# A final RMSNorm at the end of an encoder block: four output tiles scaled by token on ScalarE out of transposed banks, and the work around the last products reordered

## The chip, the core and the metric

The kernel runs on one core of one Trainium2 chip. The core has five engines with a program of their own each: TensorE (PE; its weight loads are PEld), VectorE (DVE), ScalarE (ACT), GpSimd (POOL) and SyncE (SP, which here only issues DMAs). Between engines they wait on semaphores. Sixteen DMA engines move data between HBM and the on-chip memory SBUF; matmuls write to PSUM, which the kernel uses as eight banks. The metric is the device time of one execution in microseconds (us), as the median of several runs.

## The reference

One layer of an encoder for 512 tokens of 2048 features in float32: attention and gated linear attention side by side, an output projection, a gated MLP with a convolution, and, at the end, an embedding gate and a final norm. Only this end matters here:

```python
        h = rms_norm(x, norm_ple_w[i])
        g = jax.nn.sigmoid(h @ w_ple_gate[i])
        x = x + g * (p[i] @ w_ple_proj[i])
    return rms_norm(x, final_norm_w)
```

`rms_norm` multiplies x by the inverse root of its mean square over the 2048 features of a token, and by a weight per feature. So nothing of the output can be scaled for good before the last feature of that token has been computed.

## The kernel before, in words

**Layout.** Features lie on the 128 partitions, tokens along the free dimension. Block m (0 to 7) holds features m·128 and (m+8)·128 onward as two rows s = 0, 1 of 512 tokens. The tokens are cut into a first half (`lo_half`, 0 to 255) and a second half (`hi_half`, 256 to 511).

**Products.** A projection is made of units, one for each block. Each unit is a 2x2 matrix product (two feature rows by two token halves), done with seven block products in Winograd's manner (`PRODUCTS`, L21): P1 and P2 give quarter C11 (row 0, first half), P5 and P7 C22, P6 and P3 C12 (row 0, second half), P4 C21. A float32 product is three passes of eight matmuls with rounded operands: high part by high part, high by low, low by high, 24 matmuls (`product`, L481). `prep_high` (L446) rounds the weights on ScalarE (`wh<-l`, `wh<-s`), `prep_low` (L469) takes the rest on VectorE (`wl<-`). The accumulator is a PSUM bank (accA for P1, P6, P7, P4; accB; accC for P5 and P3, banks handed on in a list by `bank`, L477). `collect` (L502) moves it into the unit's page u: a ScalarE copy for the first product of a quarter (`u<-accA`), a VectorE addition for the second (`u<-u,accC`).

**Order.** `steps` is the list of all products; in the main loop (L1262) step i first runs its agenda entries of key 0 and 1, then `prep_low` of a coming step, the product, the entries of key 2 and more, and then `collect`. Each entry is recorded through `InOrder` (L56), which holds every engine to the order of recording; that is why almost every instruction of the profile has line 64. `end` (L961) is the first of the last 14 steps: the seven products of units u6 and u7 in turn, of which the last four (P5 and P3 of each) are written out by hand behind the loop, from L1355.

**The end.** The last stage's projection is the embedding gate. A quarter is finished by `times_norm` (L947: VectorE multiplies by the earlier norm's root rb, ScalarE takes the sigmoid) and `add_gated` (L953: VectorE multiplies by the projected embedding `ppl` and adds to the residual xs, ScalarE squares into page q). The squares are added into `acc`. The blocks 0 to 5 have been stored to HBM (x3d) and are read back by `reload` (L928); `weigh` (L936) multiplies them by the final weight, two ScalarE instructions `x<-x,cols` a block, `weigh_part` (L1349) those of u6 and u7 by quarters. Final norm, for each token half: `sums_by_token` (L1301) sums acc and squares over the partitions with matmuls by ones (`ms`), `root_begin` and `root_end` (L1312, L1319) make the inverse root (`tok`: a ScalarE square root and small VectorE steps) with one token on each partition, and a diagonal matrix `dg`; `spread` (L1329) turns that into a row on all partitions by one matmul (`pb`). `finish` (L1340) multiplies a block's half by it on VectorE and writes 256 KB to the output. `keep_warm` (L1334) is matmuls whose result nobody reads (`pw`).

**Queues.** DMAs are issued by SP, ACT or POOL, each in the order of its own program; writes of the first half go by SP, of the second half by SP for odd and by ACT for even blocks.

Of the kernel before, what the change touches and what calls it, by code (L numbers as in the profile page):

```python
# [11 lines left out]
AF = mybir.ActivationFunctionType  # L12
ALU = mybir.AluOpType

P = 128
T = 512
# [25 lines left out]
def encoder_block(ctx: ExitStack, tc: tile.TileContext, A, out):  # L42
    nc = tc.nc
# [433 lines left out]
    def bank(name):  # L477
        tag = banks.pop(0)
        return tag, pp_.tile([P, T], F32, tag=tag, name=name)
# [444 lines left out]
    x3 = {}  # L924
# [3 lines left out]
    def reload(i):  # L928
        t = xtile(("R11", "R21")[i // 2], i % 2, "x3", F32)
        for j in range(2):  # L930
            m = 2 * i + j
            if m < 6:
                x3[m] = t[:, j, :].rearrange("p (s t) -> p s t", s=2)
                nc.sync.dma_start(x3[m], x3d[m])

    def weigh(m):  # L936
        for s in range(2):
            act.activation(x3[m][:, s, :], x3[m][:, s, :], AF.Copy, scale=nfin[:, m + 8 * s:m + 8 * s + 1])

    sq_page = {}  # L940
    both = slice(0, 2)
# [5 lines left out]
    def times_norm(unit, s, c):  # L947
        o = unit.o[:, s, c]
        r = rb[:, None, c].broadcast_to([P, 2, 256]) if isinstance(s, slice) else rb[:, c]
        vec.tensor_tensor(o, o, r, ALU.mult)  # L950
        act.activation(o, o, AF.Sigmoid)

    def add_gated(unit, s, c):  # L953
        o, xs = unit.o[:, s, c], unit.xs[:, s, c]
        vec.tensor_tensor(o, o, unit.pp[:, s, c], ALU.mult)
        vec.tensor_tensor(xs, xs, o, ALU.add)
        if unit not in sq_page:
            sq_page[unit] = spare("q").rearrange("p (s t) -> p s t", s=2)
        act.activation(sq_page[unit][:, s, c], xs, AF.Square)
# [2 lines left out]
    for n in range(2):  # L962
        agenda[end + 2].append((0, lambda n=n: reload(n)))
    agenda[end + 7].append((0, lambda: reload(2)))
    for m in range(4):
        agenda[end + 5 + m].append((2, lambda m=m: weigh(m)))

    for n in range(2):
        u = stages[-1].units[n - 2]
        agenda[end + 4 + 2 * n] += [(2, lambda u=u: times_norm(u, 0, lo_half))]  # L970
        agenda[end + 5 + 2 * n] += [(2, lambda u=u: add_gated(u, 0, lo_half))]
        agenda[end + 6 + 2 * n] += [(1, lambda u=u: vec.tensor_tensor(acc[:, lo_half], acc[:, lo_half], sq_page[u][:, 0, lo_half], ALU.add))]

    def mean_square(c):
        n = (c.stop - c.start) // P
# [325 lines left out]
    def sums_by_token(parts, ms=None, done=True):  # L1301

        first = ms is None
        if first:
            ms = psum_aux("ms")[:, :2]
        for n, q in enumerate(parts):
            for t in range(2):
                ten.matmul(ms[:, t:t + 1], q[:, t * P:t * P + P], ones[:, 0:1], start=first and n == t == 0,
                           stop=done and n == len(parts) - 1, skip_group_check=True)
        return ms  # L1310
# [20 lines left out]
        ten.matmul(pb, ones, dg, start=True, stop=True)  # L1331
        return pb

    def keep_warm(n):  # L1334
        t = bank("pw")
        banks.append(t[0])
        for _ in range(n):
            ten.matmul(t[1][:, :P], ones, ones, start=True, stop=True)

    def finish(c, r, ms):  # L1340
        for m in ms:
            t = x3[m][:, :, c]
            vec.tensor_tensor(t, t, r[:, None, :].broadcast_to([P, 2, 256]), ALU.mult)
            (nc.sync if m % 2 or c is lo_half else nc.scalar).dma_start(out2[m][:, :, c], t)

    u6, u7 = units[-2:]
    x3[6], x3[7] = u6.xs, u7.xs
# [1 line left out]
    def weigh_part(unit, ss, c):  # L1349
        for s in ss:  # L1350
            m = unit.u + 8 * s
            act.activation(unit.xs[:, s, c], unit.xs[:, s, c], AF.Copy, scale=nfin[:, m:m + 1])


    lo, hi = lo_half, hi_half  # L1355
    sq = lambda u, s, c: sq_page[u][:, s, c]
    ms, rs = {}, {}
    product(u6, "P5")
    times_norm(u7, 1, lo)
    collect(u6, "P5")  # L1360
    vec.tensor_tensor(acc[:, lo], acc[:, lo], sq(u6, 1, lo), ALU.add)
    add_gated(u7, 1, lo)
    product(u7, "P5")
    times_norm(u6, 1, hi)
    weigh_part(u6, range(2), lo)
    add_gated(u6, 1, hi)
    collect(u7, "P5")
    product(u6, "P3", 9, lambda: ms.update(lo=sums_by_token([acc[:, lo], sq(u7, 1, lo)])))
    times_norm(u7, 1, hi)
    w0 = root_begin(ms["lo"])  # L1370
    add_gated(u7, 1, hi)
    d0 = root_end(lo, *w0)
    weigh_part(u7, range(2), lo)
    collect(u6, "P3")
    product(u7, "P3", 10, lambda: rs.update(lo=spread(d0)))
    times_norm(u6, 0, hi)
    weigh(4)
    add_gated(u6, 0, hi)
    finish(lo, rs["lo"], (0, 1))
    collect(u7, "P3")  # L1380
    m1 = sums_by_token([acc[:, hi], sq(u6, 1, hi), sq(u7, 1, hi), sq(u6, 0, hi)], done=False)
    times_norm(u7, 0, hi)
    finish(lo, rs["lo"], (2,))
    keep_warm(8)
    add_gated(u7, 0, hi)
    act.activation(warm, ones[:, 0:1], AF.Sqrt)
    m1 = sums_by_token([sq(u7, 0, hi)], m1)
    finish(lo, rs["lo"], (3, 4))
    keep_warm(4)
    w1 = root_begin(m1)  # L1390
    d1 = root_end(hi, *w1)
    rs["hi"] = spread(d1)
    weigh(5)
    weigh_part(u6, (1, 0), hi)
    weigh_part(u7, (1, 0), hi)
    finish(lo, rs["lo"], (6,))
    finish(hi, rs["hi"], range(4))
    finish(lo, rs["lo"], (5,))
    finish(hi, rs["hi"], range(4, 8))
    finish(lo, rs["lo"], (7,))  # L1400


def _blocks(w):
# [59 lines left out]
```

## Time and profile before

| | us |
|---|---|
| median of 3 runs (2300.37 to 2307.55) | 2304.75 |
| the profiled execution | 2304.32 |
| its span, first to last instruction | 2302.6 |
| TensorE busy | 2261.4 (98%) |
| VectorE busy | 1888.0 (82%) |
| ScalarE busy | 1300.7 (56%) |
| matmuls, all engines' instructions | 18016, 44996 |

Times in rows of the profile count from the start of the span. The granted clock of TensorE is 0.99 of full on the mean. "Busy" counts the time in which an instruction is in the engine; an engine that waits for a semaphore isn't busy. A row of the timeline has start, length, engine, line, operation, what it writes and reads, shapes and the count of merged instructions, and in brackets how long the engine had stood idle before and who ended that. Instructions that follow each other overlap by some 0.1 us, so a row of two 128x512 scalings lasts less than twice one of them.

### The profile page before, as it was taken

The numbers are of one execution on the slowest core, as the hardware profiler recorded it, in microseconds if no ns is written. First come the engines' busy times: TensorE is split into PE (matmuls) and PEld (weight loads), VectorE is DVE, ScalarE is ACT, GpSimd is POOL, SyncE is SP. The second block draws the span as 40 slices with busy tenths as digits, with TensorE's granted clock in tenths as the row PEclk, the third lists the DMA queues.
The fourth block names the chain that finished last, engine by engine and source line by source line (L and its number), as shares of the span: only waits on it lengthen the run. The fifth ranks groups of instructions, "written<-read, shape, count | busy, mean of one in ns | idle before, by whom it ended". The sixth has DMA issues, their size and how long they took to land.

```text
span 2302.6 us, 44996 instructions
## 1 busy us (share of the span) xinstructions
PE 2261.4 (98%) x18016; PEld 2189.7 (95%) x18016; DVE 1888.0 (82%) x2590; ACT 1300.7 (56%) x1908; POOL 144.0 (6%) x181
## 2 busy tenths in 40 slices
PE   9999999999999999999999999999999999999996
PEld 8888889999989999999999999999999999999996
DVE  7566458998788888998888888888898787998986
ACT  6354456776565665555555555555564554656655
POOL 0000000000000100000000000000000100000000
PEclk9999999999999999999999999999999999999999
DMA  6623586667978977787878787777866967879994
GB/s 217 204 74 110 183 271 166 186 182 200 309 251 257 327 214 211 207 221 205 227 197 219 204 222 211 215 208 217 272 207 231 309 216 255 268 254 329 268 292 163
DMA packets 195569, 516.77 MB, mean 224 GB/s; under 512 B 20928, under 2 KB 72384, under 8 KB 195360
## 3 DMA queue, kind: packets, MB, share of 16 engines
q1 hardware_dynamic: 166080, 422.37, 52.5%
q0 software_dynamic: 23616, 84.95, 21.2%
q10 hardware_dynamic: 5664, 6.59, 0.8%
q8 instruction: 141, 2.31, 0.4%
q14 instruction: 68, 0.56, 0.1%
HBM read 435.18 MB, written 76.55 MB: 222 GB/s over the span
## 4 chain that ended last, share of the span: by engine, by line
PE 87%; DVE 6%; DMA 3%; ACT 3%; issue 2%; DVEq 0%; ACTq 0%; POOLq 0%; SPq 0%
PE accA L64 40%; PE accC L64 21%; PE accB L64 10%; PE v L252 3%; PE v L254 3%; PE v L253 3%; DVE wl L64 1%; DMA s<-in_w_blk 1%; PE py L64 1%; PE ptr L64 1%; PE psc L64 1%; DVE s L64 1%; DMA s<-in_w_out 1%; DVE u L64 1%; DVE xs L64 1%
## 5 line engine op out<-in xcount | busy, mean ns | idle before, releaser
L64 DVE TENSOR_TENSOR wl<-s,wh 128x1024 fp32r<-128x1024 f32 (+1 forms) x365 | 437.9, 1200 | 65.8 <-ACT wh L64 65.0
L64 ACT ACTIVATE wh<-l 128x1024 fp32r<-128x1024 f32 (+1 forms) x308 | 319.1, 1037 | 184.7 <-PE accC L64 118.0
L64 DVE TENSOR_TENSOR wl<-l,wh 128x1024 fp32r<-128x1024 f32 (+1 forms) x308 | 367.8, 1194 | 61.0 <-ACT wh L64 60.6
L64 ACT ACTIVATE wh<-s 128x1024 fp32r<-128x1024 f32 (+1 forms) x365 | 377.7, 1036 | 34.2 <-DVE s L64 15.8
L64 ACT ACTIVATE u<-accA 128x256 f32<-128x256 f32 x290 | 109.6, 378 | 365.4 <-PE accA L64 365.4
L64 DVE TENSOR_TENSOR s<-s,l 128x1024 f32<-128x1024 f32 (+1 forms) x192 | 229.7, 1196 | 8.5 <-DMA s<-in_w_blk 8.5
L64 PE MATMUL accA<-up_T,wh 128*128 128x256 f32 x1408 | 178.8, 279 | 0.0
L64 PEld LDWEIGHTS accA<-up_T,wh 128*128 128x128 f32 x1408 | 170.3, 188 | 0.0
L64 DVE SCALAR_TENSOR_TENSOR cv<-u,cw,cv 128x511 f32<-128x511 f32 (+1 forms) x176 | 131.7, 749 | 3.1
L407 POOL DMA_DIRECT2D s<-in_w_up x88 | 75.3, 856 | 787.9 <-DMA s<-in_w_up 383.6
L252 PE MATMUL v<-wv_h,h 128*128 128x512 f32 x256 | 100.2, 391 | 0.1
L254 PE MATMUL v<-wv_h,h 128*128 128x512 f32 x256 | 100.2, 391 | 0.0
L253 PE MATMUL v<-wv_l,h 128*128 128x512 f32 x256 | 99.7, 389 | 0.0
L64 PE MATMUL accA<-up_T,wl 128*128 128x256 f32 x704 | 96.6, 279 | 0.0
L64 PE MATMUL accA<-dn_T,wh 128*128 128x256 f32 x704 | 91.5, 282 | 4.1 <-ACT wh L64 4.1
L64 PE MATMUL accB<-up_R,wh 128*128 128x256 f32 x704 | 91.6, 282 | 2.0 <-DVE up_R L64 1.3
L64 PEld LDWEIGHTS accA<-dn_T,wh 128*128 128x128 f32 x704 | 86.8, 191 | 4.7 <-ACT wh L64 4.7
L64 PE MATMUL accA<-up_R,wh 128*128 128x256 f32 x704 | 89.8, 280 | 0.0
L64 PE MATMUL accC<-up_R,wh 128*128 128x256 f32 x704 | 89.4, 279 | 0.0
L64 PE MATMUL accA<-up_N,wh 128*128 128x256 f32 x704 | 89.4, 279 | 0.0
L64 PE MATMUL accC<-up_N,wh 128*128 128x256 f32 x704 | 89.4, 279 | 0.0
L64 PEld LDWEIGHTS accB<-up_R,wh 128*128 128x128 f32 x704 | 86.7, 190 | 2.7 <-DVE up_R L64 1.6
(401 smaller groups left out, 5070.6 us busy)
## 6 DMA issues: line engine op xcount, KB each, us to landing
l<-in_w_up SPq DMA_DIRECT2D x132, 512.0 KB, 5.5
s<-in_w_up SPq DMA_DIRECT2D x88, 512.0 KB, 4.9
s<-in_w_up POOLq DMA_DIRECT2D x88, 512.0 KB, 6.2
l<-in_w_dn SPq DMA_DIRECT2D x56, 448.0 KB, 5.7
l<-in_w_blk SPq DMA_DIRECT2D x36, 512.0 KB, 4.7
l<-in_w_out SPq DMA_DIRECT2D x28, 512.0 KB, 5.1
l<-in_w_dn SPq DMA_DIRECT2D x28, 512.0 KB, 5.3
s<-in_w_blk SPq DMA_DIRECT2D x24, 512.0 KB, 4.6
```

Of the source, the lines that this page charges most:

```text
L64: ins = f(*args, **kw)
L252: nc.tensor.matmul(ps[t], h1[kt][:, 0, sl], wh, start=kt == 0, stop=False)
L253: nc.tensor.matmul(ps[t], h1[kt][:, 0, sl], wl, start=False, stop=False)
L254: nc.tensor.matmul(ps[t], h1[kt][:, 1, sl], wh, start=False, stop=kt == KD - 1)
L407: nc.gpsimd.dma_start(t, src("L22" if name == "S1" else "L11"), accum_op=ALU.add)
```

## The change

The host code that calls the kernel also changes: four blocks' second token half comes back with tokens on partitions, and the host puts these pieces in place (a transposition of what was returned, with no arithmetic).

In the kernel:

1. Blocks 0 to 3, second half: instead of `finish` with the spread root, sixteen pieces of 128x128 are turned by TensorE (`turn`, with the identity; four pieces to a PSUM bank: two blocks, two rows, one quarter of the tokens), and ScalarE copies each bank to SBUF scaled by the root itself (`turned_out`; tokens lie on partitions there, so the root is a column). Two banks are turned ahead of the last ms sums, two behind.
2. In the steps `end`+4 to `end`+9, the sigmoid of the first quarter of u6 and u7 moves one step behind its VectorE multiplication, and its ScalarE square to step `end`+9; of the reloaded blocks, block 0 is weighted one row a step, block 1 at `end`+9, blocks 2 and 3 in the part written by hand.
3. The squares of all four first-half quarters go through `acc`; the first half's root follows directly on its sum, ahead of the gate of the next quarter, with the table for the square root asked for before (`warm`). The sum stands after 8 instead of 9 matmuls of u6's P3, the spread after 8 instead of 10 of u7's.
4. In the tail, `finish` of the first half is spread differently between the gate operations, block 4 and 5 move behind the second root, the table for the second square root is asked for behind the last sigmoid instead of behind the last square, the `keep_warm` matmuls go, and all writes are issued by SP.

```diff
@@ -933,9 +933,12 @@
                 x3[m] = t[:, j, :].rearrange("p (s t) -> p s t", s=2)
                 nc.sync.dma_start(x3[m], x3d[m])
 
+    def weigh_stream(m, s):
+        act.activation(x3[m][:, s, :], x3[m][:, s, :], AF.Copy, scale=nfin[:, m + 8 * s:m + 8 * s + 1])
+
     def weigh(m):
         for s in range(2):
-            act.activation(x3[m][:, s, :], x3[m][:, s, :], AF.Copy, scale=nfin[:, m + 8 * s:m + 8 * s + 1])
+            weigh_stream(m, s)
 
     sq_page = {}
     both = slice(0, 2)
@@ -962,14 +965,28 @@
     for n in range(2):
         agenda[end + 2].append((0, lambda n=n: reload(n)))
     agenda[end + 7].append((0, lambda: reload(2)))
-    for m in range(4):
-        agenda[end + 5 + m].append((2, lambda m=m: weigh(m)))
+    def gate_times(u):
+        o, xs = u.o[:, 0, lo_half], u.xs[:, 0, lo_half]
+        vec.tensor_tensor(o, o, u.pp[:, 0, lo_half], ALU.mult)
+        vec.tensor_tensor(xs, xs, o, ALU.add)
+
+    def square_first(u):
+        sq_page[u] = spare("q").rearrange("p (s t) -> p s t", s=2)
+        act.activation(sq_page[u][:, 0, lo_half], u.xs[:, 0, lo_half], AF.Square)
+
+    def add_square(u, s, c):
+        vec.tensor_tensor(acc[:, c], acc[:, c], sq_page[u][:, s, c], ALU.add)
+
 
     for n in range(2):
         u = stages[-1].units[n - 2]
-        agenda[end + 4 + 2 * n] += [(2, lambda u=u: times_norm(u, 0, lo_half))]
-        agenda[end + 5 + 2 * n] += [(2, lambda u=u: add_gated(u, 0, lo_half))]
-        agenda[end + 6 + 2 * n] += [(1, lambda u=u: vec.tensor_tensor(acc[:, lo_half], acc[:, lo_half], sq_page[u][:, 0, lo_half], ALU.add))]
+        at = end + 4 + n
+        agenda[at].append((1, lambda u=u: vec.tensor_tensor(u.o[:, 0, lo_half], u.o[:, 0, lo_half], rb[:, lo_half], ALU.mult)))
+        agenda[at + 1].append((2, lambda u=u: act.activation(u.o[:, 0, lo_half], u.o[:, 0, lo_half], AF.Sigmoid)))
+        agenda[at + 1].append((2, lambda n=n: weigh_stream(0, n)))
+        agenda[at + 2].append((1, lambda u=u: gate_times(u)))
+        agenda[end + 9].append((2, lambda u=u: square_first(u)))
+    agenda[end + 9].append((2, lambda: weigh(1)))
 
     def mean_square(c):
         n = (c.stop - c.start) // P
@@ -1331,17 +1348,11 @@
         ten.matmul(pb, ones, dg, start=True, stop=True)
         return pb
 
-    def keep_warm(n):
-        t = bank("pw")
-        banks.append(t[0])
-        for _ in range(n):
-            ten.matmul(t[1][:, :P], ones, ones, start=True, stop=True)
-
     def finish(c, r, ms):
         for m in ms:
             t = x3[m][:, :, c]
             vec.tensor_tensor(t, t, r[:, None, :].broadcast_to([P, 2, 256]), ALU.mult)
-            (nc.sync if m % 2 or c is lo_half else nc.scalar).dma_start(out2[m][:, :, c], t)
+            nc.sync.dma_start(out2[m][:, :, c], t)
 
     u6, u7 = units[-2:]
     x3[6], x3[7] = u6.xs, u7.xs
@@ -1350,6 +1361,25 @@
         for s in ss:
             m = unit.u + 8 * s
             act.activation(unit.xs[:, s, c], unit.xs[:, s, c], AF.Copy, scale=nfin[:, m:m + 1])
+
+
+    def turn(n):
+        t = bank("turned")[1]
+        for b in range(4):
+            m, s = 2 * (n % 2) + b // 2, b % 2
+            c = slice(256 + n // 2 * P, 384 + n // 2 * P)
+            ten.transpose(t[:, b * P:b * P + P], x3[m][:, s, c], ident)
+        return t
+
+    def turned_out(n, t, r):
+        if n % 2 == 0:
+            turned_page[:] = [spare("turned")]
+        o = turned_page[0][:, n % 2 * T:n % 2 * T + T]
+        act.activation(o, t, AF.Copy, scale=r[:, n // 2:n // 2 + 1])
+        m = 2 * (n % 2)
+        nc.sync.dma_start(out2[m + n // 2][:, :, hi_half], o.rearrange("p (s t) -> p s t", s=2))
+
+    turned_page = []
 
 
     lo, hi = lo_half, hi_half
@@ -1357,47 +1387,60 @@
     ms, rs = {}, {}
     product(u6, "P5")
     times_norm(u7, 1, lo)
+    for u in (u6, u7):
+        add_square(u, 0, lo)
+    add_square(u6, 1, lo)
+    weigh(3)
+    add_gated(u7, 1, lo)
     collect(u6, "P5")
-    vec.tensor_tensor(acc[:, lo], acc[:, lo], sq(u6, 1, lo), ALU.add)
-    add_gated(u7, 1, lo)
     product(u7, "P5")
     times_norm(u6, 1, hi)
-    weigh_part(u6, range(2), lo)
+    weigh(2)
+    add_square(u7, 1, lo)
     add_gated(u6, 1, hi)
     collect(u7, "P5")
-    product(u6, "P3", 9, lambda: ms.update(lo=sums_by_token([acc[:, lo], sq(u7, 1, lo)])))
+    act.activation(warm, ones[:, 0:1], AF.Sqrt)
+    product(u6, "P3", 8, lambda: ms.update(lo=sums_by_token([acc[:, lo]])))
+    w0 = root_begin(ms["lo"])
+    d0 = root_end(lo, *w0)
     times_norm(u7, 1, hi)
-    w0 = root_begin(ms["lo"])
+    weigh_part(u6, range(2), lo)
     add_gated(u7, 1, hi)
-    d0 = root_end(lo, *w0)
-    weigh_part(u7, range(2), lo)
     collect(u6, "P3")
-    product(u7, "P3", 10, lambda: rs.update(lo=spread(d0)))
+    product(u7, "P3", 8, lambda: rs.update(lo=spread(d0)))
     times_norm(u6, 0, hi)
     weigh(4)
+    finish(lo, rs["lo"], (0,))
     add_gated(u6, 0, hi)
-    finish(lo, rs["lo"], (0, 1))
+    weigh_part(u7, range(2), lo)
+    finish(lo, rs["lo"], (1,))
     collect(u7, "P3")
-    m1 = sums_by_token([acc[:, hi], sq(u6, 1, hi), sq(u7, 1, hi), sq(u6, 0, hi)], done=False)
+    m1 = sums_by_token([acc[:, hi], sq(u6, 1, hi), sq(u7, 1, hi)], done=False)
+    turned = [turn(n) for n in range(2)]
+    m1 = sums_by_token([sq(u6, 0, hi)], m1, done=False)
     times_norm(u7, 0, hi)
+    act.activation(warm, ones[:, 0:1], AF.Sqrt)
     finish(lo, rs["lo"], (2,))
-    keep_warm(8)
     add_gated(u7, 0, hi)
-    act.activation(warm, ones[:, 0:1], AF.Sqrt)
     m1 = sums_by_token([sq(u7, 0, hi)], m1)
-    finish(lo, rs["lo"], (3, 4))
-    keep_warm(4)
+    turned += [turn(n) for n in range(2, 4)]
+    finish(lo, rs["lo"], (3,))
     w1 = root_begin(m1)
     d1 = root_end(hi, *w1)
     rs["hi"] = spread(d1)
+    weigh_part(u6, (1, 0), hi)
+    finish(lo, rs["lo"], (6,))
+    for n in range(2):
+        turned_out(n, turned[n], w1[3])
+    finish(hi, rs["hi"], (4,))
     weigh(5)
-    weigh_part(u6, (1, 0), hi)
     weigh_part(u7, (1, 0), hi)
-    finish(lo, rs["lo"], (6,))
-    finish(hi, rs["hi"], range(4))
-    finish(lo, rs["lo"], (5,))
-    finish(hi, rs["hi"], range(4, 8))
-    finish(lo, rs["lo"], (7,))
+    finish(lo, rs["lo"], (4,))
+    finish(hi, rs["hi"], (6,))
+    for n in range(2, 4):
+        turned_out(n, turned[n], w1[3])
+    finish(hi, rs["hi"], (5, 7))
+    finish(lo, rs["lo"], (7, 5))
 
 
 def _blocks(w):
@@ -1459,4 +1502,13 @@
         encoder_block(tc, A, out)
     r = run_bass_kernel_spmd(nc, [{"in_" + n: a for n, a in arrays.items()}], core_ids=[0])
     y = r.results[0]["out_0"]
+
+    y = y.copy()
+    h = y[:, :, 256:].copy()
+    for n in range(4):
+        for j in range(2):
+            m, t = 2 * (n % 2) + j, n // 2
+            place = h[2 * (n % 2) + t + 8 * j].reshape(P, 2, P)
+            for b in range(2):
+                y[m + 8 * b, :, 256 + t * P:384 + t * P] = place[:, b].T
     return np.ascontiguousarray(y.reshape(D, T).T).reshape(1, T, D)
```

## The prediction

> **What bounds the kernel now.** The page comes first: TensorE is busy 98% of the span. The built programs hold the same instructions in the same order on every engine until 2249 us, so the change is decided in the last 54 us. I read that stretch in the timeline (start us, us, engine, line, operation, out<-in, count, idle before it and who ended it), then the waits, then the writes. The last weight steps:
>
> ```profile
> 2247.47 2.03 PE L64 MATMUL accA<-pg_N,wh 128*128 128x256 f32 x16
> ...
> 2250.27 2.03 PE L64 MATMUL accA<-pg_N,wh 128*128 128x256 f32 x16
> ...
> 2252.84 0.42 ACT L64 ACTIVATE u<-u 128x256 f32<-128x256 f32 x1 [3.09 <-DVE u L64]
> 2253.16 1.04 ACT L64 ACTIVATE last<-s 128x1024 fp32r<-128x1024 f32 x1
> 2254.11 0.36 ACT L64 ACTIVATE u<-accA 128x256 f32<-128x256 f32 x1
> ...
> 2254.37 1.05 ACT L64 ACTIVATE wh<-s 128x1024 fp32r<-128x1024 f32 x1
> ...
> 2254.53 2.14 PE L64 MATMUL accA<-pg_T,wh 128*128 128x256 f32 x16 [1.29 <-ACT u L64]
> 2255.32 1.33 ACT L64 ACTIVATE x<-x,cols 128x512 f32<-128x512 f32 x2
> ```
> ```profile
> 2269.12 2.04 PE L64 MATMUL accC<-pg_N,wh 128*128 128x256 f32 x16
> ```
> ```profile
> PE accA L64 <- ACT u L64: 3.7, 4, 1.6
> ```
>
> A product is 24 matmuls and takes 2.80 us undisturbed (2247.47 to 2250.27; 0.117 each). The five from 2250.27 to 2269.12 take 18.85 instead of 14.0, so 4.85 us are lost. The waits view (us, times, longest) puts 3.7 of it on four waits for ScalarE's eviction u<-accA; the rest is its counting from a modelled matmul end (0.28 long where the next may follow at 0.117) and slower restarts. The eviction itself is short, 0.36. It stands in line: ScalarE idled 3.09 us on a sigmoid that waited for VectorE, with `last` and the eviction behind it.
>
> The rest of the tail:
>
> ```profile
> 2276.69 3.23 PE L64 MATMUL accC<-pg_R,last 128*128 128x256 f32 x25
> ...
> 2277.83 1.28 ACT L64 ACT_TABLE_LOAD   x1
> 2279.12 0.26 ACT L64 ACTIVATE tok<-ms,epst 128x2 f32<-128x2 f32 x1
> 2279.42 0.16 DVE L64 TENSOR_SCALAR tok<-ms 128x2 f32<-128x2 f32 x1 [2.06 <-ACT tok L64]
> ...
> 2281.06 0.48 DVE L64 TENSOR_SCALAR dg<-ident,tok 128x128 f32<-128x128 f32 x2
> ...
> 2281.60 0.70 PE L64 MATMUL pb<-dg,ones 128*128 128x256 f32 x2 [1.68 <-DVE dg L64]
> ...
> 2283.80 0.50 PE L64 MATMUL ms<-ones,acc 128*128 128x1 f32 x4
> ...
> 2284.18 1.28 DVE L64 TENSOR_TENSOR x<-x,pb 128x512 f32<-128x512 f32 x2
> ...
> 2285.37 0.41 DVE L64 TENSOR_TENSOR u<-u,accC 128x256 f32<-128x256 f32 x1
> ...
> 2286.28 0.42 ACT L64 ACTIVATE u<-u 128x256 f32<-128x256 f32 x1 [1.40 <-DVE u L64]
> ...
> 2288.10 1.28 ACT L64 ACT_TABLE_LOAD   x1
> ...
> 2289.50 0.24 ACT L64 ACTIVATE tok<-ms,epst 128x2 f32<-128x2 f32 x1
> ...
> 2290.24 0.36 DVE L64 SCALAR_TENSOR_TENSOR tok<-tok 128x2 f32<-128x2 f32 x2
> ...
> 2291.74 0.37 SPq L1344 DMA_DIRECT2D out<-xs  x1
> ```
>
> Three things are to be seen. TensorE stands in the middle of its last product until the first half's root is spread (`pb`): its 25 matmuls from 2276.69 are issued by 2279.61, `pb` starts at 2281.60, 1.99 later. A table load sits bare on the path ahead of each square root. The second root is ready at 2290.60 (2290.24 + 0.36), and everything behind it is output. The span ends 12.0 us after that:
>
> ```profile
> span 2302.6 us, 44996 instructions
> ```
> ```profile
> 2294.00:2300.00 6.00, 0.00 (x0) 0.00 (x0) 3.97 (x7) 0.00 (x0) 0.00 (x0) 0.50 1.02 342
> 2286.00:2287.00 1.00, 1.00 (x11) 1.00 (x10) 1.00 (x3) 0.42 (x1) 0.00 (x0) 1.00 1.01 343
> ```
> ```profile
> out<-x ACTq DMA_DIRECT2D x1, 256.0 KB, 2.2
> ```
> ```profile
> 2298.00 1.06 SPq L1344 DMA_DIRECT2D out<-xs  x1
> ```
> ```profile
> out<-xs SPq DMA_DIRECT2D x1, 256.0 KB, 3.6
> ```
>
> The last two columns of a window are the DMA share and GB/s. From 2294 the 16 DMA engines are full (1.02) at 342 GB/s: 262,144 bytes take 0.767 us. So the writes, not VectorE, set the end there. The third row is the write issued at 2292.63, landing 2.2 us later; nine more at 0.767 give 2301.7, and the last landed at 2298.00 + 3.6 = 2301.6. Then 1.0 us of closing.
>
> **The change part by part.** I carry the new order of each engine's instructions forward from 2250.27 on this trace's clock, each with its row's duration and 0.035 to 0.055 us between engines (ScalarE u 2252.84 + 0.42, and so on). The old order carried the same way has its second root 0.16 us early.
>
> *ScalarE's queue in the steps.* The sigmoid now comes a step after its product with 0.61 of scaling instead of 1.22, and the squares and three blocks' scaling go behind the last evictions. Each step holds wh 0.95 (2254.37 to 2255.32), sigmoid 0.32 (2252.84 to 2253.16) or `last` 0.95, one scaling 0.61 (1.33 for two overlapping ones) and an eviction 0.26: under 2.80. What is late next is the last weight loads, issued and landing so:
>
> ```profile
> 2243.98 0.45 SPq L404 DMA_DIRECT2D l<-in_w_ple_gate  x1
> ```
> ```profile
> l<-in_w_ple_gate SPq DMA_DIRECT2D x1, 512.0 KB, 11.9
> ```
> ```profile
> 2247.59 0.33 SPq L404 DMA_DIRECT2D l<-in_w_ple_gate  x1
> ```
> ```profile
> l<-in_w_ple_gate SPq DMA_DIRECT2D x1, 512.0 KB, 10.8
> ```
>
> They land at 2255.89 and 2258.39; nothing ahead of them in their queue moves. wh then starts at 2255.93 and sigmoid, half a scaling and eviction end at 2258.19; TensorE needs that bank at 2250.27 + 3 x 2.80 = 2258.67, a slack of 0.48 (the smallest is 0.4, a step earlier). After the second, wh 0.95, `last` 0.95 and the eviction end at 2260.66, needed at 2261.47. So no product waits, and accC starts at 2264.27: **-4.85**.
>
> *Behind the steps.* The moved squares (0.32 each) and scalings (1.22 a block) now stand before ScalarE's last eviction, which ends at 2267.38; behind it VectorE runs rb, three chained additions to acc (0.45 each, as the two dependent steps from 2285.37 to 2286.28), two gate operations and only then the eviction of accC, done 2270.23. TensorE is ready for the same bank at 2264.27 + 5.60 = 2269.87: **+0.4**, a new wait.
>
> *First root.* The sum of the last block now goes through acc, so two of four ms matmuls go (0.45 at four records of 0.112). The table load is asked for early, but in ScalarE's order it stands behind 2 x 0.61 of scaling and a square: 2272.7 to 2274.0, tok at 2274.1. VectorE's root has no gate operations inside (two of 0.41, in the 2.12 from 2279.42 to 2281.54), so dg ends at 2275.7 and `pb` starts at 2275.8. TensorE is there at 2270.29 + 32 x 0.117 + 0.45 = 2274.5: 1.3 of idling stay of 1.99. Together with the 0.45, about **-1.1**. The last product ends at 2278.3 against 2283.80: -5.5.
>
> *Second root.* VectorE's two `finish` products (0.60 apart) are split around the gate, one still ahead of the last eviction: 0.3 later relative to TensorE. The table load now starts behind the sigmoid, beside VectorE's two gate operations, and the square waits for it: sigmoid 2281.06, load 2281.5 to 2282.8, square to 2283.3, ms 0.5, tok 2284.0. From sigmoid to tok that is 2.93 instead of 3.22: -0.3. The root is ready at 2285.1: -5.5.
>
> *Writes.* Four of VectorE's products with the spread root go (0.60 each); ScalarE scales the turned banks with the root itself, without dg and `pb`. Nearest row, the same operation out of PSUM with a column as scale:
>
> ```profile
> L258 ACT ACTIVATE Vg<-v,rtok 128x512 f32<-128x512 f32 x8 | 5.3, 691 | 3.2 <-PE v L254 3.2
> ```
>
> The first turned write is issued at 2285.09 + 0.04 + 0.69 + 0.04 = 2285.86. But 12 writes are left instead of 11, since block 4's first half moved behind the root. Landing 2.2, then 11 x 0.767 = 8.44, then 1.0: the span ends at 2297.5, **-5.1** in all. VectorE's seven products (0.60) and ScalarE's eight scalings (4.4 us) each feed the queue faster than it drains, so they cost nothing; without that cover, ScalarE's last two (0.59 each) would be added. The ACT queue's four writes go to SP, which needs 0.6 a write (0.37 and a wait) against 0.767: nothing. The 16 transposes (records of 0.275, 0.112 apart as the ms ones) fill TensorE's idle time.
>
> *Keep-warm gone.* Twelve fillers of 2 records go. Rows of their tile, last ones and those of the cold start:
>
> ```profile
> L64 PE MATMUL pw<-ones x24: 275/275/356, 2285.5 to 2289.5; 128*128 128x128 f32 x24
> L81 PE MATMUL pw<-ones x22: 421/421/579, 1.2 to 5.9; 128*128 128x128 f32 x22
> ```
> ```profile
> 2276.00:2284.00 8.00, 6.33 (x53) 6.07 (x51) 4.59 (x17) 6.40 (x13) 0.00 (x0) 1.00 0.01 2
> ...
> 2292.90:2293.40 0.50, 0.00 (x0) 0.00 (x0) 0.50 (x2) 0.00 (x0) 0.00 (x0) 0.74 1.00 340
> ```
>
> The granted clock (third column from the end) stayed at 1.00 across the 1.68 us of idling before `pb`, and fell (0.74, then the 0.50 of the window from 2294) 1.3 us after TensorE's last work at 2291.87. The change leaves TensorE idle for 2.3 us ahead of the last ms pair, between these two cases. A gain is excluded, for that pair waited for ScalarE's square and not for fillers. The upper bound is the pair and `pb` at half speed, 0.45 and 0.7, of which `pb` lies off the path, since the turned writes go first. I take nothing, as in the nearer row, the idling that was followed by more work. The Trainium skill (TensorE: Matmul & The Clock Gate, "What's actually happening") speaks against this part: an idle window of about 3.4 us, free-running, halves the clock. By that rule the sum would be -4.6 if such a window ends just ahead of the pair, else -5.1. The trace agrees on the halving; the window's length is in none of these rows.
>
> The profiled execution took 2304.32 (span 2302.6), 0.43 below the median of 2304.75. It gives 2304.32 - 5.1 = 2299.2; from the median, 2299.6. I say 2299.5.
>
> **The rivals.**
> (a) *Late loads take the wait's place.* The last loads take 10.8 and 11.9 us to land in a full DMA stretch; each 1 us later than here costs 1 less 0.48 to 0.8. Two late: +1.5, 2301.0. For: the steps are now paced by them. Against: their queue is unchanged.
> (b) *Cold clock.* As above, with the sums before it too: 2300.0 to 2300.4. For: the fillers go. Against: the 1.68 us that the clock survived, and little of the path is TensorE's there.
> (c) *One queue is too slow, and the kernel gets slower.* All twelve writes go through SP. The last issue took 1.06 instead of 0.37. From 2285.86 + 2.2 to 2301.6 - that is today's last landing - 13.5 us are there for 11 writes: from 1.23 us a write on, the change loses. At 1.5: 11 x 0.73 = 8.1 more, 2307.6. Against: at 2286 SP alone moved 343 GB/s.
> (d) *More is won.* If the 0.4 and 1.3 of TensorE idling go as well: 2297.8.
> (e) *Nothing comes of it*, since the turned tiles arrive late: ScalarE's third is issued 3.9 us behind the root, when six writes of 0.767 are still ahead. No price.
>
> **How the numbers follow.** Forecast 2299.5 (2298 to 2301) 0.62; (a) 0.14, (b) 0.10, (c) 0.05, (d) 0.07, (e) 0.02. Range 2296.0 to 2303.0: the forecast, (a), (b) and (d), and about 2 us either way for a median of runs that spread over 7.2 us (2300.37 to 2307.55). Within 0.3% of before, about what a measurement can tell from no change, is 2297.8 to 2311.7: the forecast is 1.7 above the lower end, so by that spread a third of it and most of (d) fall below. Faster 0.26, within 0.70, slower 0.04 (the part of (c) beyond 1.9 us a write).
>
> **What would show it.** Right: no wait of accA for u above 0.2; accC's first matmul near 2264.3; `pb` with about 1.0 idle before it; first turned write at 2285.9; DMA share 1.0 from there to the last landing at 2296.5. Wrong: waits of wh for in_w_ple_gate (a), ms records of 0.4 and a clock of 0.5 before the second root (b), DMA share well under 1 with writes queued on SP (c).

## The result, and the profile after

| | before | after |
|---|---|---|
| median | 2310.86 us (22 runs, 2299.14 to 2315.35) | 2302.05 us (22 runs, 2290.98 to 2307.13) |
| after to before | | 0.9974 (95%: 0.9962 to 0.9986), about 6.0 us (the two medians alone differ by 8.8) |
| the profiled execution, its span | 2304.32, 2302.6 | 2290.98, 2289.3 |

The ratio lies clear of 1: the change makes the kernel faster by 0.26%. The forecast took 5.1 us off the profiled execution and so had the size. The two spans differ by 13.3 us, but most of that isn't the change's. A **landmark** tells the two apart, the start of the second product accA<-pg_N, up to which both programs are the same: 2250.27 before, 2242.49 after. So 7.8 us were there before the change begins (the last section says from where), and the **tail**, from the landmark to the end of the span, went from 52.3 to 46.8: -5.5. All that follows counts from the landmark.

TensorE's products in the timeline of after:

```profile
2242.49 2.03 PE L64 MATMUL accA<-pg_N,wh 128*128 128x256 f32 x16
...
2256.49 2.03 PE L64 MATMUL accC<-pg_N,wh 128*128 128x256 f32 x16
```

Five products in 14.00 us instead of 18.85. The waits view of TensorE, from 2240 to the end (us, times, longest), has no accA any more:

```profile
PE ms L64 <- ACT q L64: 2.4, 1, 2.4
PE pb L64 <- DVE dg L64: 0.9, 1, 0.9
```

The rest of the tail in the timeline, with the two roots and the first write behind the second:

```profile
2264.69 1.28 ACT L64 ACT_TABLE_LOAD   x1
...
2267.76 0.70 PE L64 MATMUL pb<-dg,ones 128*128 128x256 f32 x2 [0.95 <-DVE dg L64]
...
2270.20 0.50 PE L64 MATMUL ms<-ones,acc 128*128 128x1 f32 x4
...
2272.09 0.89 ACT L64 ACTIVATE xs<-xs,cols 128x256 f32<-128x256 f32 x2
2272.10 0.41 DVE L64 TENSOR_TENSOR u<-u,accC 128x256 f32<-128x256 f32 x1
...
2272.36 0.50 PE L64 MATMUL ms<-ones,q 128*128 128x1 f32 x4
2272.55 0.42 DVE L64 TENSOR_TENSOR u<-u,rb 128x256 f32<-128x256 f32 x1
2272.89 0.68 DVE L64 TENSOR_TENSOR x<-x,pb 128x512 f32<-128x512 f32 x1
2273.01 0.42 ACT L64 ACTIVATE u<-u 128x256 f32<-128x256 f32 x1
...
2275.30 1.01 PE L64 MATMUL ms<-ones,q 128*128 128x1 f32 x4 [2.43 <-ACT q L64]
...
2277.10 0.36 DVE L64 SCALAR_TENSOR_TENSOR tok<-tok 128x2 f32<-128x2 f32 x2
...
2278.20 0.37 SPq L1380 DMA_DIRECT2D out<-turned  x1
```

And windows of the same stretch (the granted clock is the third column from the end, then DMA share and GB/s):

```profile
2272.80:2274.00 1.20, 0.07 (x1) 0.00 (x0) 1.17 (x4) 1.16 (x3) 0.00 (x0) 1.00 0.61 218
2274.00:2275.30 1.30, 0.00 (x1) 0.01 (x1) 0.96 (x2) 1.23 (x3) 0.00 (x0) 0.91 0.55 197
2275.30:2276.30 1.00, 1.00 (x5) 1.00 (x6) 0.00 (x0) 0.00 (x0) 0.00 (x0) 0.50 0.41 144
...
2282.00:2288.40 6.40, 0.00 (x0) 0.00 (x0) 1.56 (x3) 0.00 (x0) 0.00 (x0) 0.50 0.95 328
```

Three things are to be seen. The last product ends at 2270.20 (27.7 behind the landmark; 33.5 before), and TensorE still idles 0.95 before pb. The clock falls to 0.50 just ahead of the last ms pair, whose four records take 1.01 instead of 0.50. Behind the second root (2277.46) DMA is again what binds: twelve writes from 2278.20, the last landing at 2288.4.

### The profile page after: what moved, and what is told of

Same layout as the page of the kernel before. It is cut to its first block, busy times and chain, and to the rows that moved or that the text cites. A ratio compares the mean times of both kernels' runs of the same rounds, so it can differ in the third digit from the quotient of the medians.

```text
span 2289.3 us, 44978 instructions
## 1 busy us (share of the span) xinstructions
PE 2255.1 (99%) x18004; PEld 2183.3 (95%) x18004; DVE 1885.3 (82%) x2587; ACT 1302.1 (57%) x1913; POOL 143.6 (6%) x181
## 4 chain that ended last, share of the span: by engine, by line
PE 84%; DVE 7%; DMA 4%; ACT 3%; issue 2%; ACTq 0%; DVEq 0%; SPq 0%; POOLq 0%
PE accA L64 39%; PE accC L64 20%; PE accB L64 10%; PE v L252 3%; PE v L254 3%; PE v L253 3%; DVE wl L64 2%; DMA l<-in_w_dn 1%; DVE s L64 1%; DMA s<-in_w_dn 1%; PE py L64 1%; PE ptr L64 1%; PE psc L64 1%; DMA wo_T<-mix_T 1%; DMA s<-in_w_blk 1%
## 5 line engine op out<-in xcount | busy, mean ns | idle before, releaser
L64 ACT ACTIVATE wh<-s 128x1024 fp32r<-128x1024 f32 (+1 forms) x365 | 377.9, 1036 | 34.8 <-DVE s L64 18.5
L64 PEld LDWEIGHTS accA<-up_T,wl 128*128 128x128 f32 x704 | 88.5, 188 | 0.0
```

The lines of the kernel that those rows point to most:

```text
L64: ins = f(*args, **kw)
```

## The experiments

Times alone don't part edits of 1 us here: with 10 or 12 runs the interval is 0.1 to 0.2% (2 to 4 us) to each side, e8 has five runs, and e9, e10 and e14 one each. The verdicts go by the profile, one execution of each kernel, in stages of the tail (us behind the landmark; all figures from the timelines, "root" is the end of the last small VectorE step on tok; "last load" is the landing of the last `l<-in_w_ple_gate`):

| run | last load | accC starts | first root | last product ends | second root | writes behind it | tail |
|---|---|---|---|---|---|---|---|
| before | 8.1 | 18.85 | 30.8 | 33.5 | 40.3 | 11 | 52.3 |
| after | 7.9 | 14.00 | 24.7 | 27.7 | 35.0 | 12 | 46.8 |
| e1 steps alone | 8.2 | 14.00 | 26.6 | 30.8 | 36.2 | 11 | 48.3 |
| e2 steps undone | 8.3 | 18.83 | 29.6 | 32.7 | 39.9 | 12 | 51.8 |
| e3 not turned | 8.2 | 14.00 | 25.0 | 28.0 | 35.3 | 12 | 48.6 |
| e8 first root undone | 8.0 | 14.00 | 26.2 | 29.0 | 35.3 | 12 | 47.1 |
| e4 fillers | 7.4 | 14.00 | 24.2 | 27.2 | 34.0 | 12 | 45.9 |
| e5 two writes early | 7.9 | 14.00 | 24.7 | 27.8 | 35.0 | 10 | 45.8 |
| e6 = e4 + e5 | 7.8 | 14.00 | 24.6 | 27.6 | 34.5 | 10 | 44.9 |
| e7 two queues | 8.2 | 14.00 | 25.0 | 28.0 | 35.0 | 12 | 47.2 |
| e9 gate in the wait | 7.9 | 14.00 | 25.3 | 28.4 | 33.7 | 12 | 45.6 |
| e10 product later | 7.8 | 14.00 | 24.6 | 27.6 | 34.8 | 12 | 46.6 |
| e14 = e10 + scaling later | 8.1 | 14.00 | 24.9 | 27.9 | 34.2 | 12 | 46.0 |
| e12 loads first | 5.7 | 14.00 | 23.4 | 26.5 | 33.7 | 12 | 45.5 |
| e13 four edits | 5.4 | 14.00 | 24.1 | 27.1 | 33.1 | 10 | 43.5 |
| e15 same, 4 fillers | 5.6 | 14.00 | 24.0 | 27.1 | 32.4 | 10 | 42.8 |

**The parts one by one.** e1 is before with the new agenda of the steps alone, as in the diff, and in the part written by hand the additions and scalings that it moves there:

```diff
     product(u6, "P5")
     times_norm(u7, 1, lo)
+    for u in (u6, u7):
+        add_square(u, 0, lo)
+    weigh(3)
     collect(u6, "P5")
...
     times_norm(u6, 1, hi)
+    weigh(2)
```

> The kernel before with part 2 of the change alone: the new order of the sigmoids, squares and scalings in the steps, and with it the two additions to acc and the scalings of blocks 2 and 3 in the part written by hand. The tail, from the start of the second accA<-pg_N product to the end of the span, was 52.33 us before (2250.27 to 2302.6) and 46.81 after (2242.49 to 2289.3). Theory: the four waits of accA for ScalarE go and no other wait comes: accC's first matmul 14.0 us behind the landmark instead of 18.85, and of the 4.85 some 0.5 is given back at the first root, because ScalarE now has 4.3 us more to do ahead of its table load where it had 3.8 us of idling: tail 48.0 (47.5 to 48.5). Rival, late loads: a wait of wh for in_w_ple_gate takes the place, tail 49 to 50. Rival, the first root takes all: VectorE and ScalarE, not TensorE, set when pb is there, tail 51 or more with pb idle above 4.

Measured: tail 48.3, ratio 0.9991 (0.998 to 1.0003). The steps give 4.85, and 0.7 is given back: the first root stands 12.6 behind accC's start instead of 11.9. Neither rival. Here the granted clock is 0.50 from 2280.6 to 2283.9, behind 2.35 us of idling before pb, and the last product ends 4.2 behind the first root instead of 2.8; yet the second root stands 9.7 behind the first, in before 9.6. So here the end of the last product isn't what sets it.

e2 undoes the same in after: before's agenda lines are put back, and in the part written by hand

```diff
-    for u in (u6, u7):
-        add_square(u, 0, lo)
     add_square(u6, 1, lo)
-    weigh(3)
...
-    weigh(2)
```

> The kernel after with part 2 of the change alone undone: sigmoids, squares and scalings stand in the steps as before. Theory: the waits of accA for u come back, 4.85 in five products, but ScalarE and VectorE have less to do behind the steps, so that the 0.95 of TensorE idling before pb and the 0.17 before the last product go: tail 46.81 + 4.85 - 1.1 = 50.5 (50.0 to 51.7). Rival: the steps' order is worth little beside the other parts, tail under 48.5.

Measured: tail 51.8, just above the range; nothing of the expected 1.1 comes back, and the steps are worth 5.0 of the 5.5. The rival falls.

e3 undoes the turning:

```diff
-    for n in range(2):
-        turned_out(n, turned[n], w1[3])
-    finish(hi, rs["hi"], (4,))
+    finish(hi, rs["hi"], (0, 1, 4))
...
-    for n in range(2, 4):
-        turned_out(n, turned[n], w1[3])
-    finish(hi, rs["hi"], (5, 7))
+    finish(hi, rs["hi"], (2, 3, 5, 7))
```

> The kernel after with part 1 of the change undone: no block is turned, the second half of blocks 0 to 3 goes through VectorE and the spread root, in the places where the turned ones stood; the host gets it as before. Theory: the first write behind the root is xs of u6, 0.47 later than the first turned one, the next has to wait for pb (2279.25) and a product of 0.6, so it is issued at 2279.95 and DMA runs out in between; from there the writes bound again: +1.0 (0.5 to 1.5), tail 47.8. Rival, it is worth nothing, for the writes bound anyway: tail 46.8. Rival, VectorE's four products at 0.6 stand on the path: +2.4, tail 49.2.

Measured: from the second root to the end 13.3 instead of 11.8. The timeline of e3, behind that root:

```profile
2284.64 1.22 PE L64 MATMUL pb<-dg,ones 128*128 128x256 f32 x2 [1.72 <-DVE dg L64]
...
2285.26 0.37 SPq L1355 DMA_DIRECT2D out<-xs  x1
2285.90 2.48 DVE L64 TENSOR_TENSOR x<-x,pb 128x512 f32<-128x512 f32 x4 [0.72 <-PE pb L64]
2286.61 2.16 SPq L1355 DMA_DIRECT2D out<-x  x4
```

VectorE waits for pb (1.22 at half clock), and the second write comes 1.35 behind the first, where a transfer takes 0.7: DMA runs dry. So turning is worth 1.5 here, the upper end of what was expected (1.0, with this slow pb already in it); the tail, 48.6, holds 0.3 more from a later root. The first write comes 0.45 later behind the root than in after and the gap behind it costs some 0.8 more. The ten writes behind the gap land 0.77 apart where the last ten of after land 0.74 apart, nearly 0.4 in all; why is open.

e8 undoes the first root's part:

```diff
-    act.activation(warm, ones[:, 0:1], AF.Sqrt)
-    product(u6, "P3", 8, lambda: ms.update(lo=sums_by_token([acc[:, lo]])))
-    w0 = root_begin(ms["lo"])
-    d0 = root_end(lo, *w0)
+    product(u6, "P3", 9, lambda: ms.update(lo=sums_by_token([acc[:, lo], sq(u7, 1, lo)])))
     times_norm(u7, 1, hi)
-    weigh_part(u6, range(2), lo)
+    w0 = root_begin(ms["lo"])
     add_gated(u7, 1, hi)
+    d0 = root_end(lo, *w0)
+    weigh_part(u6, range(2), lo)
```

> The kernel after with the first root's part (3) undone: the last block's sum goes through two more ms matmuls at position 9, the table isn't asked for ahead, VectorE's gate operations stand inside the root again and the spread is at position 10. Theory: the table load ends some 0.3 later behind the sigmoid, VectorE's two gate operations add 0.8, so pb comes 1.1 later and TensorE, which idled 0.95 before it, idles 1.8; with the ms matmuls +1.2 (0.9 to 1.5), tail 48.0. Rival: the last product's end doesn't set the second root, so nothing of it arrives: tail 46.8 to 47.1.

Measured: the first root is 1.5 and the last product 1.2 later, but the second root only 0.3, and the tail 0.4, where 1.2 was expected. The rival holds: between the roots after needs 10.3 us, e8 9.1. What the earlier first root brings, the gate that VectorE now does behind it takes back.

**The clock, the writes, the queue.** e4 and e5:

```diff
+    keep_warm(8)
     m1 = sums_by_token([sq(u7, 0, hi)], m1)
```
```diff
-    finish(lo, rs["lo"], (3,))
+    finish(lo, rs["lo"], (3, 4, 6))
     w1 = root_begin(m1)
```

> The kernel after with eight of the filler matmuls put back, ahead of the last ms pair (no filler behind it). In the profile of after the granted clock fell to 0.50 during 2.43 us of TensorE idling ahead of that pair, whose four records took 1.01 us instead of 0.50. Theory (the prediction's rival b, cold clock): with the fillers the clock is 1.00 at the pair, its records take 0.50, the second root stands 34.45 us behind the landmark (the second accA<-pg_N product) instead of 34.96, and the tail is 46.3 instead of 46.78. Rival: the clock's falling hangs on the moment, not on this idling, and the pair takes 1.0 all the same: tail 46.8. Rival: the fillers themselves delay the pair: root beyond 35.0, tail above 46.8.

> The kernel after with the first half of blocks 4 and 6 finished ahead of the second root, in the 1.68 us in which VectorE waits for it, instead of behind it: 10 writes are left behind the root instead of 12. Theory: behind the root the writes bound, some 0.73 us each by the landings of after; two fewer, less what their transfers still take from the first turned write, 1.0 to 1.5 us: tail 45.5 (45.3 to 45.8), root unmoved at 34.96. Rival: VectorE's two products come into the root's way (root beyond 35.5), tail 46.3 or more. Rival: VectorE and ScalarE, not the writes, set the end: tail 46.6 to 46.8.

> The two together: fillers ahead of the last ms pair, and blocks 4 and 6 finished ahead of the second root. Theory: the gains add, 0.5 and 1.0 to 1.5, unless the earlier root comes into VectorE's products (0.1): tail 45.0 (44.7 to 45.3), some 1.8 faster than after and 7.3 than before. Rival: with the root earlier the transfers of the early writes are still under way, and the second gain shrinks: tail 45.5.

e4's timeline and a window of it:

```profile
2276.01 2.03 PE L64 MATMUL pw<-ones 128*128 128x128 f32 x16
2278.59 0.61 PE L64 MATMUL ms<-ones,q 128*128 128x1 f32 x4 [0.54 <-ACT q L64]
2279.05 1.07 PE L64 MATMUL turned<-ident,x 128*128 128x128 f32 x8
```
```profile
2278.00:2279.00 1.00, 0.46 (x5) 0.41 (x5) 0.25 (x1) 0.52 (x3) 0.00 (x0) 1.00 0.59 209
```

The clock stays at 1.00, the pair takes 0.61. The way between the roots is 9.9 instead of 10.3: the cold clock cost 0.4. The other 0.5 that e4's tail is shorter comes from its last load, which landed 0.5 earlier. e5 takes 1.0 off behind the root, e6 1.4, 44.9 in all: both as expected.

e7, and the like in `turned_out`:

```diff
-            nc.sync.dma_start(out2[m][:, :, c], t)
+            (nc.sync if m % 2 or c is lo_half else nc.scalar).dma_start(out2[m][:, :, c], t)
```

> The kernel after with the second half's writes of even blocks issued by ScalarE's queue again, as before the change, the others by SP. Theory: the 16 DMA engines bound, not the queue, so nothing changes: tail 46.8 (46.6 to 47.0). Rival (the prediction's rival c, one queue is too slow): with two queues the writes land closer than the 0.73 us of after and the tail is 46.3 or less. Rival: the issues stand in ScalarE's way ahead of its scalings: tail 47.2 or more.

Measured: tail 47.2, above the range. 0.3 of that is a later load, and behind the root it takes 12.1 us instead of 11.8. One queue isn't what binds: with two the writes land 0.75 us apart, in after 0.72. The third rival shows instead: ScalarE, which issues in the order of its program, stands 1.66 us ahead of a scaling until VectorE has finished a product to be written, and VectorE then stands 1.18 for that scaling.

**What paces the tail.** In every run with the new steps, the first root and the loads as in after, that root stands 16.8 us behind the landing of the last load (24.7 - 7.9; e4 24.2 - 7.4; e7 25.0 - 8.2), whatever else is changed, and in between TensorE waits 0.3 at most, for VectorE (e7). Rows of after's timeline:

```profile
2248.00 1.06 ACT L64 ACTIVATE wh<-l 128x1024 fp32r<-128x1024 f32 x1 [2.12 <-DMA l<-in_w_ple_gate]
...
2249.09 1.23 DVE L64 TENSOR_TENSOR wl<-l,wh 128x1024 fp32r<-128x1024 f32 x1 [0.67 <-ACT wh L64]
...
2250.46 1.06 ACT L64 ACTIVATE wh<-l 128x1024 fp32r<-128x1024 f32 x1 [0.21 <-DMA l<-in_w_ple_gate]
...
2251.56 1.23 DVE L64 TENSOR_TENSOR wl<-l,wh 128x1024 fp32r<-128x1024 f32 x1 [0.44 <-ACT wh L64]
...
2256.55 0.42 ACT L64 ACTIVATE u<-u 128x256 f32<-128x256 f32 x1 [1.64 <-DVE u L64]
```

VectorE waits for the loads' high parts (0.67, 0.44) and then has a backlog, for which ScalarE waits in turn (1.64). e12 takes the transfers of blocks 2 and 3 from ahead of these loads:

```diff
-    for n in range(2):
-        agenda[end + 2].append((0, lambda n=n: reload(n)))
+    agenda[end + 2].append((0, lambda: reload(0)))
+    agenda[end + 5].append((0, lambda: reload(1)))
```

> The kernel after, with the reading back of blocks 2 and 3 (two transfers of 512 KB) issued behind the last two loads of in_w_ple_gate instead of ahead of them. Theory: in every profile with the new step order the first root stands 16.80 us behind the landing of the last of these loads (7.36 to 8.20 behind the landmark), with no wait of TensorE in between: the loads pace VectorE, which has no slack from there to the root. They land 2.5 us earlier (5.2 to 5.6), and VectorE takes back the 0.67 and 0.44 that it stood idle for their high parts: first root at 23.6 (23.3 to 24.0) instead of 24.69, tail 45.7. Rival: ScalarE's order sets the first root, squares and scalings ahead of its last evictions: root at 24.7, tail 46.8. Rival: the blocks come too late for their scaling: tail above 47.

The last load in e12, in its timeline and in the list of issues (KB, us to landing), and the same in after:

```profile
2248.24 0.33 SPq L404 DMA_DIRECT2D l<-in_w_ple_gate  x1
```
```profile
l<-in_w_ple_gate SPq DMA_DIRECT2D x1, 512.0 KB, 8.4
```
```profile
2239.81 0.33 SPq L404 DMA_DIRECT2D l<-in_w_ple_gate  x1
```
```profile
l<-in_w_ple_gate SPq DMA_DIRECT2D x1, 512.0 KB, 10.6
```

It lands at 5.7 instead of 7.9, the first root comes at 23.4, 1.3 earlier, and the tail is 45.5. Theory right, both rivals fall. TensorE shows it too, but later: its wait for VectorE before pb, 0.95 in after, is gone, and from 2248 on its waits view has one line:

```profile
PE ms L64 <- ACT q L64: 2.4, 1, 2.4
```

**Between the roots.** e9 takes u7's gate into VectorE's wait; e10 moves two products; e14 is e10 with ScalarE's scaling moved too:

```diff
+    times_norm(u7, 1, hi)
     act.activation(warm, ones[:, 0:1], AF.Sqrt)
     product(u6, "P3", 8, lambda: ms.update(lo=sums_by_token([acc[:, lo]])))
+    o, xs = u7.o[:, 1, hi], u7.xs[:, 1, hi]
+    vec.tensor_tensor(o, o, u7.pp[:, 1, hi], ALU.mult)
+    vec.tensor_tensor(xs, xs, o, ALU.add)
     w0 = root_begin(ms["lo"])
     d0 = root_end(lo, *w0)
-    times_norm(u7, 1, hi)
+    act.activation(sq_page[u7][:, 1, hi], xs, AF.Square)
     weigh_part(u6, range(2), lo)
-    add_gated(u7, 1, hi)
```
```diff
-    finish(lo, rs["lo"], (1,))
     collect(u7, "P3")
...
-    finish(lo, rs["lo"], (2,))
+    finish(lo, rs["lo"], (1,))
     add_gated(u7, 0, hi)
...
-    finish(lo, rs["lo"], (3,))
+    finish(lo, rs["lo"], (2, 3))
```
```diff
-    weigh_part(u7, range(2), lo)
     collect(u7, "P3")
...
     weigh_part(u7, (1, 0), hi)
+    weigh_part(u7, range(2), lo)
```

> The kernel after, with u7's second-half gate (multiplication by rb, sigmoid, multiplication and addition on VectorE) taken from behind the first root to VectorE's wait for it; the table load for the first square root then stands behind that sigmoid. Theory: since the change the second root is set by VectorE's chain, first root, gate, collect, gate, collect, and not by TensorE's last product. So the first root comes 0.45 later and the last product with it (0.4), but the chain behind it is 1.2 shorter: from first root to second 9.0 us (8.8 to 9.2) instead of 10.27, tail 0.8 shorter: 46.0, if the last load of in_w_ple_gate lands 7.9 us behind the landmark as in after; where it lands by more or less, the tail moves by the same. Rival: TensorE's last product sets the second root, which then comes 0.4 later: tail 47.2.

> The kernel after, with one VectorE product (the first half of block 1 by the spread root, 0.6) moved from ahead of the last collect to behind it, and block 2's behind the last gate. Theory as before: VectorE's chain sets the second root, so that it comes 0.5 earlier (from first root to second 9.75 instead of 10.27), tail 46.2 at the same load landing. Rival: TensorE's last product sets it, root and tail stay (46.8).

> The run with one VectorE product moved behind the last collect, and in addition ScalarE's scaling of u7's first half (two instructions, 0.80) moved from ahead of the last sigmoid to behind the second root. In that run the product brought 0.13 between the roots (10.14 us instead of 10.27) where 0.5 was expected. Theory now: the last sigmoid stood behind VectorE and behind ScalarE's scalings alike (VectorE done at 2272.97, ScalarE at 2272.98 in after), so neither edit alone brings anything, and both together bring 0.4: from first root to second 9.7 (9.6 to 9.8), tail 46.2 at a load landing of 7.8. Rival: something else sets the second root, and it stays at 10.1; tail 46.6.

e9: from root to root 8.4 instead of 10.3, where 9.0 was expected; some 0.4 of it is the clock, which stayed up there. The last product ends 0.7 later than in after and the second root comes 1.2 earlier, so the rival falls. e10 is a miss: 10.1 where 9.75 was expected. The rows of after above say why: VectorE's step on rb ends at 2272.97, but ScalarE's scaling xs<-xs,cols ends at 2272.98, and the sigmoid at 2273.01 stands behind both. e14 takes both away: 9.3, of which 0.4 by the clock, which stayed up, and 0.45 by the edit. So no one engine sets the second root; VectorE's and ScalarE's queues hold the same sigmoid up alike.

**The best version.** e13 joins e4, e5, e9 and e12. e15 is e13 with

```diff
-    keep_warm(8)
+    keep_warm(4)
```

> The kernel after with four of the edits: fillers ahead of the last ms pair, blocks 4 and 6 finished ahead of the second root, u7's gate in VectorE's wait for the first root, and blocks 2 and 3 read back behind the last weight loads. Theory: on the tail of the first two together, 44.91, the gate takes another 0.8 and the loads 1.1: 43.0 (42.5 to 43.6), 9.3 less than before the change and 3.8 less than after. Rival: from here TensorE's last product binds, and half of the last two gains is lost: 44.0.

> The kernel with the four edits (43.52), with four fillers instead of eight: there the eight ran until 0.85 us after the last square, and so held up the last ms pair. Theory: without that the pair starts 0.3 behind the square as in the other runs, the second root comes 0.7 earlier: tail 42.8 (42.6 to 43.1), 9.5 less than before the change and 4.0 less than after. Rival: with fewer fillers the clock falls ahead of the pair, 0.4 is lost again: tail 43.2 or more.

e13, 43.5, is at the upper end. Its timeline shows what it lost:

```profile
2285.86 2.03 PE L64 MATMUL pw<-ones 128*128 128x128 f32 x16
2287.73 0.50 PE L64 MATMUL ms<-ones,q 128*128 128x1 f32 x4
```
```profile
2286.48 0.40 ACT L64 ACTIVATE q<-xs 128x256 f32<-128x256 f32 x1
```

The square is done at 2286.88, the fillers hold TensorE until 2287.7. With four fillers (e15) the tail is 42.8, 9.5 less than before and 4.0 less than after; the median is 2298.81 (12 runs), the ratio to before 0.9963 (0.9951 to 0.9975). That interval and after's (0.9962 to 0.9986) overlap, and e6, with a tail of 44.9, has a ratio of 0.9983: by times alone no version is shown to be faster than after, and the 4.0 stands on the profile.

## Why the prediction was right, and where it wasn't

- **The step that failed** is the last, how the numbers follow: "Within 0.3% of before, about what a measurement can tell from no change", with 0.70 on it and 0.26 on faster. The forecast itself was a ratio of 0.9977, and a difference of 5 us can be told from none: with 22 runs of each kernel the interval is 0.12% to each side, so the measured 0.26% lies within that 0.3% and clear of no change. The spread of three runs (7.2 us) was taken for the uncertainty of a median. Before's median also came out at 2310.86, 6 us above that of the three runs, which moved the bound of 0.3% with it.
- **The waits of accA** (-4.85) were right to the hundredth: accC starts at 14.00, as carried (2264.27 on before's clock), and 5.0 of the tail's 5.5 hang on this part (e2).
- **"What is late next is the last weight loads"** was right, the slack of 0.48 was TensorE's alone. VectorE and ScalarE have none from these loads to the first root, so a later load lengthens the tail (e12, and the scatter of 0.8 us over the runs). TensorE shows that only later and under another name, as waits for VectorE: up to 0.3 in its products behind accC's start and 0.95 before pb. Rival (a)'s sign, a wait of wh for in_w_ple_gate, is there (2.12), though the load came no later than before (7.9 against 8.1): the sign doesn't tell the rival from the forecast.
- **The new wait** of +0.4 was there, and under 0.2. **First root**: pb idles 0.95 (about 1.0 expected in this column; the 1.3 counts from the last issue, where it is 1.1), the last product ends at 27.7 (28.0 expected). But the -1.1 was booked as if it arrived: undone, the second root moves by 0.3 (e8). The root came out nearly right, it seems, because the carried order of all engines holds both effects; the text credited them to the wrong place.
- **Second root**: expected at 34.8, measured at 35.0 in spite of the cold clock, +0.4, which the prediction took as nothing. Rival (b), at 0.10, came true in this profile: the clock fell 0.2 us ahead of the pair (0.91 on the mean of the 1.30 us before it), after 2.2 us of idling.
- **Writes**: the first turned one was expected at 35.6 and came at 35.7; twelve landed in 10.2 us where 2.2 + 8.4 = 10.6 were expected. That VectorE's and ScalarE's work there "cost nothing" held. The turning itself had no price of its own in the sum: it is 1.5 us, for without the turned writes DMA runs dry until pb and a product are done (e3). Of blocks 4 and 5, which the change is said to move behind the second root, only block 4's first half moved; block 5's stood there before. Rival (c), one slow queue, fell (e7). Rival (d) had more to be won from TensorE's idling; the further 4.0 us of e15 come from the clock, the writes, the gate and the loads, and pb still idles 0.5 there.
- **The total**, -5.5 where -5.1 was added up, is in part luck: the last product 0.3 earlier and the writes 0.4 faster outweigh the 0.4 of the clock.

## What to carry to other kernels

When TensorE's waits go, look which engine's queue now runs without idling from the last transfer to the end: a late load can lengthen a kernel while TensorE's waits name another engine, many us later. A gain on one chain is booked at the point where it meets the others, and moving one of two instructions that hold up the same third brings next to nothing (0.13 us here). Whether a small forecast can be measured depends on the number of runs, not on the spread of a few.

## What the runs showed of the hardware

**TensorE has two rates at a granted clock of 1.00.** In 400 us in which it is busy throughout, with the same instructions, the windows view counts 3431 matmuls in after (and in before), 3399 in e14:

```profile
1200.00:1600.00 400.00, 400.00 (x3431) 400.00 (x3430) 345.44 (x413) 210.57 (x286) 34.98 (x41) 1.00 0.77 213
```
```profile
1200.00:1600.00 400.00, 400.00 (x3399) 400.00 (x3398) 343.17 (x405) 208.35 (x282) 34.64 (x41) 1.00 0.77 209
```

That is 0.9%. Of the 16 profiles 7 have the one count and 9 the other (3398 or 3399); the landmark lies at 2242.5 to 2250.3 in the first and at 2250.9 to 2258.9 in the others. All the programs are the same there, so it is none of the edits, and it isn't the chip alone: of e1, e2, e3 and e8, which ran on one chip, two have each count. What causes it stays open.

**Half-clock stretches make up the rest.** One in before, and the same time in after:

```profile
361.00:368.00 7.00, 4.99 (x40) 4.56 (x39) 5.79 (x16) 2.94 (x7) 0.00 (x0) 1.00 0.65 160
368.10:371.40 3.30, 3.30 (x18) 3.30 (x17) 3.16 (x13) 3.30 (x9) 0.00 (x0) 0.50 0.02 5
```
```profile
368.10:371.40 3.30, 3.30 (x38) 3.10 (x36) 3.09 (x18) 3.30 (x11) 0.00 (x0) 1.00 0.11 12
```

TensorE runs 18 matmuls instead of 38, some of which are other and smaller ones, since after is some 2 us ahead there. Ahead of the landmark before has six such stretches of 3.4 us, after one; at up to 1.7 us each (half of 3.4) that is the size of the 7.8 us by which the two profiles differ there. The other profiles with the count of 3431 lie in line: with 2, 4, 4, 4 and 5 stretches their landmarks lie at 2244.1, 2245.4, 2246.2, 2246.3 and 2248.8. The Trainium skill (TensorE: Matmul & The Clock Gate, "What's actually happening") has a free-running window of that length, and the trace agrees with it on length and halving; by the page it takes an idle window, but here TensorE had worked part of it (4.99 of the 7 us ahead of this one, 1.41 of the last 3.42). That it runs free shows in before, where the clock falls at 368.02, 572.83 and 811.76: 60 and 70 times 3.413 us apart. In the tail it fell behind windows of 3.41 us with 1.21 us of work (after) and 1.90 (e8) and stayed up behind one with 2.49 (e9); but it also fell behind one with 2.72 (e12), so where the bound lies is open.
